# Attention scores in three float32r products: the lower parts of the keys on all 128 partitions, and one set of weights for both products of a score block

## The chip, the cores and the metric

The kernel runs on one core of a Trainium2 chip. The metric is the device time of one execution in microseconds (us). A profile is one execution taken by the hardware profiler; its times run from the first instruction of the program.

## What is computed

A backbone of two layers over 512 latent tokens and 256 context tokens of width 1024. Layer 0 mixes tokens by grouped-query attention (8 query heads, 2 key heads, 64 channels a head) beside a gated recurrence; layer 1 is an RWKV-7 mixer; each layer ends in a squared-ReLU MLP. The change lies in layer 0's attention alone:

```python
def attend(q, k, v):
    s = jnp.einsum('bqhgd,bkhd->bhgqk', q, k).astype(F32) * HEAD_DIM ** -0.5
    p = jax.nn.softmax(s, axis=-1).astype(v.dtype)
    return jnp.einsum('bhgqk,bkhd->bqhgd', p, v)

k_all = jnp.concatenate([kch, klh], axis=1)      # context keys, latent keys
att_l = blocked_attend(qlh, k_all, v_all)        # latents read all 768 keys
att_c = attend(qch, kch, vch)                    # context reads its 256 keys
```

## The kernel before

**Number format.** TensorE works here on float32r, whose products keep fewer bits than float32. So a float32 operand x is split into a high part hi (x as float32r) and a low part lo = x - hi, and a product of two such operands is made as a sum of products of parts. The dense products take three: hi hi, lo hi and hi lo (`mm3`, L270 to L276).

**Queries and keys.** `heads0` (L557) norms and rotates them, and its `stack` (L596 to L605) makes the parts. A tile of the stream holds two heads, one on partitions 0 to 63, the other on 64 to 127; `half(s)` is that half. For queries `stack` makes one tile a head, with hi on the head's own half of the partitions and lo, sent there by a DMA (L604), on the other half. For keys (`dup`) it makes one tile a head with hi on both halves, and one tile `kl` for both heads with each head's lo on its own half. ScalarE writes hi (L602), VectorE subtracts for lo (L603), SyncE's queue issues the DMAs (L604), and also those of the rotation (L591) that follow in the program.

**Scores.** `attention` (L625) goes through 12 units: four pairs of heads times three groups of query tiles (two groups of latents with 768 keys, one of context with 256 keys). Its generator `probs` (L632) makes four score tiles a unit (two heads, two query tiles of 128). A score tile is a PSUM tile `mm` with 768 or 256 columns, in segments of 512 and 256 columns, and a segment takes two products:

```python
self.mm(ps[:, c0:c1], q[j][s][:, qc], kd[s][:, c0:c1], True, False)   # L641
self.mm(ps[:, c0:c1], q[j][s][r, qc], kl[r, c0:c1], False, True)      # L642
```

The first contracts 128 rows (hi and lo of the queries with hi of the keys), the second the 64 rows of one half (hi with lo). In the trace both stand on L47, the helper `mm`: the first as `mm<-kq`, `128*128`, the second as `mm<-kl,kq`, `64*128` (rows times columns of the array). There are two `mm` tiles in PSUM (`mm2`, L71). A score tile is then read by VectorE for its row maximum (L645), by ScalarE for the exponential (L649), which is the last to read it, and the probabilities are scaled on GpSimd (L652).

**Values.** `values` (L656) transposes the probabilities (L663, `128*128`), copies them out (L666 on VectorE, L668 on ScalarE in turn) and multiplies them by the values (L671, in the trace on L47 as `aux<-pT,v`, `128*64`). The program interleaves the values of one unit with the scores of the next, and after each unit takes a step of other work (L688): a 1 MB block of modulation weights `ada_w` (L134, into one of two buffers `wst`), multiplied in small products (L136, `aux<-wst,cpad`, `128*32`). The compiler's scheduler orders each engine's instructions when the program is built; at run time each engine works its list in that order.

Before attention the last tiles of the input projection run on TensorE (`mm<-hhi,whi` and the like); after it the output projection (`mm<-mxh,whi`) starts.

Of the kernel before, what the change touches and what calls it, by code (L numbers as in the profile page):

```python
# [7 lines left out]
F32 = mybir.dt.float32  # L8
F32R = mybir.dt.float32r
# [6 lines left out]
P = 128  # L16
D = 1024
KT = 8
NL = 512
NC = 256  # L20
NT = NL + NC
# [13 lines left out]
class Net:  # L35
# [21 lines left out]
    @contextmanager  # L57
    def pool(self, name, side=None):
        """A pool for one part of the program; sb() allocates in the innermost."""
        old = self.sp  # L60
        with self.tc.tile_pool(name=name, bufs=1, side=side, reuse_waits="tile") as self.sp:
            yield self.sp
        self.sp = old
# [14 lines left out]
    def consts(self):  # L78
# [22 lines left out]
        # silu(c) = c/2 (1 + tanh(c/2)), the 2 rows padded with zeros to 32 columns  # L101
# [53 lines left out]
    def fill(self, n=1):  # L155
        """Emit n steps of the work that is waiting to be interleaved."""
        for _ in range(n):
            while self.todo:
                try:
                    next(self.todo[0])  # L160
                    break
                except StopIteration:
                    self.todo.pop(0)
# [5 lines left out]
    def ada_scale(self, l, j):  # L169
        """A = g (1 + scale) of norm j of layer l, for latents and context."""  # L170
        t = self.cp.tile([P, 2, KT], F32, name="A%d%d" % (l, j))
        for v in range(2):
            self.nc.vector.scalar_tensor_tensor(
                t[:, v, :], self.mod[l][:, v, (3 * j + 1) * KT:(3 * j + 2) * KT], 1.0,
                self.vec[:, VEC["g%d%d" % (l, j)], :], op0=OP.add, op1=OP.mult)
        self.A[l, j] = t
# [58 lines left out]
    def norm_split(self, l, j, ctx, parts, rb, tmp, ready=False):  # L235
        """In steps of a tile."""
# [33 lines left out]
    def mm3(self, ps, w, h, cols, first, last):  # L270
        """ps += w^T h by the three products of the parts."""
        (wh, wl), (hh, hl) = w, h
        c0, c1 = cols
        self.mm(ps, wh, hh[:, c0:c1], first, False)
        self.mm(ps, wh, hl[:, c0:c1], False, False)
        self.mm(ps, wl, hh[:, c0:c1], False, last)  # L276

    def gemm_tile(self, w, hi, lo, ctx, nk=KT):
        """One 128-row tile of (h W)^T for all tokens."""
# [7 lines left out]
    def gemm_pair(self, ws, hi, lo, ctx):  # L287
        """Two such tiles side by side, as h's tiles become ready."""
# [13 lines left out]
    def gemm_residual(self, l, chunk, blocks, hi, lo, pool, side, late, dest=None):  # L302
        """x += gate (h W), and the sums for the next norm. The context of the tiles from late on comes last, and between
        them what follows for the latents (side). These go to dest as well."""
# [22 lines left out]
    def mlp(self, l, ctx, parts, hpool):  # L327
        """parts: the normed stream, in a pool that is closed here. After layer 0's, the sums of squares of the
        stream are there."""
# [40 lines left out]
    def rg_consts(self):  # L370
# [5 lines left out]
        # softplus(-lam) = max(-lam, 0) + log1p(z), z = exp(-|lam|); log1p(z) = 2 atanh(z / (2 + z))  # L376
# [52 lines left out]
    def in_proj0(self, m, rb):  # L429
# [33 lines left out]
        # a tile of recurrent channels, then one of queries, four times  # L463
# [12 lines left out]
        with self.pool("m0pr"):  # L476
# [4 lines left out]
            # output gate of the recurrence  # L481
# [11 lines left out]
    def recurrence(self, i, ps, gw, m):  # L493
        """A tile of recurrent channels: centred convolution; gates, one scan per direction."""
# [62 lines left out]
    def heads0(self, qg, vT, pst):  # L557
        """Norm, rotation and float32r parts of queries, keys and values."""
# [6 lines left out]
        # 1 / rms of the heads, by token  # L565
# [30 lines left out]
        def stack(dup, x):  # L596
            """By head: parts of a half of the rows, with hi again (dup) or lo below; and lo where it was."""
            hs = [sb([P, NT], F32R, "kq", 10) for _ in range(2)]
            lo = sb([P, NT], F32R, "kl") if dup else self.sb([P, NT], F32, "tmp", 3, pool=self.mi).bitcast(F32R)
            for s, t in enumerate(hs):  # L600
                h, o = self.half(s), self.half(1 - s)
# [3 lines left out]
            return hs, lo  # L605
# [19 lines left out]
    def attention(self, rec, heads, mx):  # L625
        """By two tiles of queries of two heads; the heads' products side by side on the array."""
# [3 lines left out]
        groups = ((0, 0, NT), (2, 0, NT), (4, NL, NC))      # first query tile, first key, keys  # L630

        def probs(j, g, pr):  # L632
            qt0, kc0, nk = g
            for s in range(2):
                r, head = self.half(s), 2 * j + s
                for qt in range(qt0, qt0 + 2):
                    ps = self.mm2()
                    qc = slice(qt * P, qt * P + P)
                    for c0, c1, _ in self.segs(True):
                        if c0 >= kc0:  # L640
                            self.mm(ps[:, c0:c1], q[j][s][:, qc], kd[s][:, c0:c1], True, False)  # L641
                            self.mm(ps[:, c0:c1], q[j][s][r, qc], kl[r, c0:c1], False, True)  # L642
# [60 lines left out]
    def tm_norm_pool(self):  # L703
        self.rctx.append(self.wpool("l1n"))
        p = self.rctx[-1].__enter__()
        self.nb = self.sb([P, KT, NT], F32, "nb1", pool=p)       # sum of the neighbours
        self.rb = self.sb([P, NT], F32, "rb", pool=p)

    def tm_norm(self, seg, *tag):
        """The modulated norm, in place of the stream, and the sums of its tokens' neighbours."""  # L710
# [12 lines left out]
    def tm_project(self, keep):  # L723
        """The context's norm, token shift and the projections, and from them by pair of heads what the scan takes: to
        DRAM."""
# [23 lines left out]
        # two sets of parts; one is partly where the values' inputs will be  # L749
# [18 lines left out]
        # the low-rank sides of decay, in-context rate and gate, beside the keys  # L768
# [30 lines left out]
        # keys and their heads' norms  # L799
# [43 lines left out]
    def tm_pairs(self, vin, lw):  # L843
        """By pair of heads: loads (A), low rank products by direction (B0, B1), exponentials (C0, C1), products (D0, D1)
        and L (E0, E1). Then the values' projection, with the first inverses."""
        nc = self.nc
        with self.psum("l1e") as self.pq:
# [24 lines left out]
            # decays by step: the backward direction's a step ahead  # L872
# [24 lines left out]
    def tm_values(self, vin):  # L897
        """Values by token, to DRAM."""
        nc = self.nc
        xh, xl = [self.sb([P, NT], F32R, "vxh", KT, pool=self.vp) for _ in range(KT)], []  # L900
        for b in range(4):
# [4 lines left out]
            if b == 0:  # L906
                # an input's lower part in place of the input before
# [4 lines left out]
            for t0, tn in ((4, 2), (0, 4)) if b else ((0, 4), (4, 2)):  # L912
                ps = self.ps([P, 1024], "mmb", 2, pool=self.pq)
                for kt in range(KT):
                    for t in range(tn):
                        c = slice((t0 + t) * P, (t0 + t + 1) * P)
                        o = ps[:, 256 * t:256 * t + 256]
                        self.mm(o, xh[kt][:, c], wh[:, kt], kt == 0 and t % 2 == 0, False)    # two tiles share a bank
# [8 lines left out]
    def tm_prep_consts(self):  # L927
# [3 lines left out]
        # decayed keys come from k (s1 - s0 t), t = -tanh  # L931
# [5 lines left out]
    # A chunk has 64 tokens; 0-7 are latents, 8-11 context. In the scan, for direction d, the rows of a chunk's values  # L937
    # (by token) are on partitions 64 d on; those of its U, and its keys, queries and state by channel, on the other
    # half; the two heads of a pair lie side by side. The delta rule's queries are kk / sqrt 2, its keys -(tanh + 1)
    # times that; U is scaled to match.  # L940
    def tm_prep(self, kt, lw):
        """A pair of heads' decayed keys, queries and their products."""
# [13 lines left out]
        # normalised kk  # L956
# [8 lines left out]
        for d in range(2):  # L965
# [15 lines left out]
            # decay since the chunk's start and its inverse, for the sum before the token too  # L981
# [9 lines left out]
        for d in range(2):  # L991
# [20 lines left out]
            if d:  # L1012
                # the bonus' factor of v by token: r . (k both directions) r_k
# [35 lines left out]
    def tm_feed(self, i, KB=None, W=None):  # L1049
        """What step i needs besides the inverses, in pieces."""  # L1050
# [20 lines left out]
        for g in range(4):  # L1071
# [10 lines left out]
            if i:  # L1082
                # queries to go with the state
# [15 lines left out]
    def tm_invert(self, j):  # L1099
        """(I - L)^-1 of the chunks of steps 2 j and 2 j + 1: the diagonal 32 x 32 blocks by forward substitution,  # L1100
        chunks on partitions. The backward direction's L is upper triangular; its transpose goes the same way."""
        nc = self.nc
        XT = self.XT[j] = self.sb([P, 2, 2, KT, 64], F32, "XT", 3, pool=self.ip)      # step, head of a pair, pair, token
# [20 lines left out]
    def tm_below(self, j):  # L1124
        """The block below the diagonal: X22 L21 X11. In pieces, two for each of the two steps."""
# [30 lines left out]
    def tm_step(self, i, kt):  # L1156
        """Step i of the scan of a pair of heads."""
# [60 lines left out]
    def tm_post(self, l, parts=1):  # L1218
        """Group norm (but its shift), scale and bonus of chunks l and 7 - l, for all heads; from Y, by token, to Y, by channel."""
# [40 lines left out]
    def tm_masks(self):  # L1260
# [8 lines left out]
        self.GL = sb([P, 32, 32], F32, "GL")   # token, unit  # L1269
# [3 lines left out]
    def tm_scan(self):  # L1273
# [5 lines left out]
        # queries by channel, with zeros for the other direction's  # L1279
# [65 lines left out]
    def out1_ahead(self):  # L1345
        """Loads of the gate's and half of the output's weights, to where inverses were."""
# [22 lines left out]
    def out1(self, wo):  # L1369
        """Gate, output projection and residual: the inner 256 tokens, then the outer ones."""  # L1370
# [54 lines left out]
def layout(inp):  # L1425
    """The arrays of setup_inputs() as the program takes them: reordered, nothing computed."""
# [29 lines left out]
    # a head's channels: the first of every rotary pair, then the second  # L1456
# [20 lines left out]
    # layer 1  # L1477
# [3 lines left out]
    up = np.zeros((2, HD, 2, 2, D), np.float32)     # zeros in the rows of the other direction  # L1481
# [43 lines left out]
```

## Time and profile before

| | us |
|---|---|
| device time, three runs | 2335.08, 2324.70, 2331.64 |
| median | 2331.64 |
| span of the profiled execution | 2334.9 |
| TensorE busy in it | 2069.8 (89%) |
| VectorE, ScalarE, GpSimd busy | 1188.5, 870.0, 525.8 |
| attention, first to last score product | 239.70 to 391.8 |

The span of the profiled execution is 0.1% above the median of the runs. "PE" is TensorE, "PEld" its weight loads, "DVE" VectorE, "ACT" ScalarE, "POOL" GpSimd, "SPq" SyncE's queue. The duration that the trace gives for a matmul includes a modelled drain that lies under the next one; what a matmul takes of TensorE's time is the distance from its start to the start of the next. PEclk is the granted clock of TensorE as a share of 2.4 GHz, so that 0.50 is the lower level, 1.2 GHz.

### The profile page before, as it was taken

How to read it: one execution, taken by the hardware profiler on the slowest of the kernel's cores; microseconds unless marked ns; L12 is line 12 of the kernel's file. 1: busy time of each engine (PE TensorE's matmuls, PEld its weight loads, DVE VectorE, ACT ScalarE, POOL GpSimd, SP SyncE). 2: the span in 40 equal slices, each digit the busy share in tenths (PEclk: the TensorE clock that was granted, in tenths of full speed). 3: DMA queues.
4: the chain of work that ended last, by engine and by line, in shares of the span. 5: the costliest groups of instructions: out<-in, count | busy, mean ns of one | idle time of the engine just before them, and what ended most of it. 6: DMA issues, size and time to landing. Idle time of an engine off the chain costs nothing. (4 is left out here: it accounts for less than half of the span.)

```text
span 2334.9 us, 37318 instructions
## 1 busy us (share of the span) xinstructions
PE 2069.8 (89%) x15710; PEld 1639.0 (70%) x15710; DVE 1188.5 (51%) x1835; ACT 870.0 (37%) x1333; POOL 525.8 (23%) x530
## 2 busy tenths in 40 slices
PE   6888999999999999997987768578877878999999
PEld 3567445778888888875764558567756667788887
DVE  4557455262222222328648998638766584333333
ACT  3664344142121221317645542245534432332331
POOL 0123222011010110105005872660510130210210
PEclk8999789999999999998998778789888889999999
DMA  7324221123333212212224568286465330223222
GB/s 274 126 99 135 102 108 55 54 86 132 108 109 116 83 55 73 95 44 74 91 90 169 215 238 160 52 140 115 73 102 110 74 118 19 91 92 103 95 91 90
DMA packets 231784, 248.54 MB, mean 106 GB/s; under 512 B 52416, under 2 KB 209472, under 8 KB 225216
## 3 DMA queue, kind: packets, MB, share of 16 engines
q1 hardware_dynamic: 229568, 240.91, 35.5%
q0 software_dynamic: 896, 3.15, 0.4%
q8 instruction: 123, 2.02, 0.4%
q10 hardware_dynamic: 1152, 2.10, 0.2%
q14 instruction: 45, 0.37, 0.1%
HBM read 200.82 MB, written 41.94 MB: 104 GB/s over the span
## 5 line engine op out<-in xcount | busy, mean ns | idle before, releaser
L264 ACT ACTIVATE whi<-wst 128x1024 fp32r<-128x1024 f32 x160 | 169.2, 1059 | 583.6 <-PE mm L47 566.2
L47 PE MATMUL mm<-hhi,whi 128*128 128x512 f32 (+1 forms) x992 | 347.2, 357 | 14.5 <-ACT hhi L250 7.5
L47 PE MATMUL mm<-hlo,whi 128*128 128x512 f32 (+1 forms) x992 | 352.7, 356 | 2.2 <-DVE hlo L251 2.1
L47 PE MATMUL mm<-hhi,wlo 128*128 128x512 f32 (+1 forms) x992 | 350.3, 354 | 0.0
L265 DVE TENSOR_TENSOR wlo<-wst,whi 128x1024 fp32r<-128x1024 f32 x160 | 200.1, 1253 | 253.6 <-ACT whi L264 250.8
L345 POOL TENSOR_TENSOR mp<-mr 128x768 f32<-128x768 f32 (+1 forms) x64 | 109.9, 1718 | 841.5 <-ACT mr L344 841.5
L47 PE MATMUL mm<-ahi,wlo 128*128 128x512 f32 (+1 forms) x704 | 253.0, 359 | 0.0
L47 PE MATMUL mm<-ahi,whi 128*128 128x512 f32 (+1 forms) x704 | 252.9, 360 | 0.0
L47 PE MATMUL mm<-alo,whi 128*128 128x512 f32 (+1 forms) x704 | 252.6, 359 | 0.0
L300 DVE SCALAR_TENSOR_TENSOR Xt<-mm,mod,Xt 128x512 f32<-128x512 f32 (+1 forms) x112 | 70.6, 652 | 337.0 <-PE mm L47 337.0
L47 PEld LDWEIGHTS mm<-hhi,whi 128*128 128x128 f32 x992 | 188.2, 191 | 52.8 <-ACT hhi L250 9.5
L47 PEld LDWEIGHTS mm<-hlo,whi 128*128 128x128 f32 x992 | 189.1, 191 | 31.3 <-DVE hlo L251 5.7
L47 PEld LDWEIGHTS mm<-hhi,wlo 128*128 128x128 f32 x992 | 188.8, 190 | 29.1 <-issue 1.7
L47 PEld LDWEIGHTS mm<-ahi,whi 128*128 128x128 f32 x704 | 132.2, 188 | 28.1 <-issue 6.7
L47 PEld LDWEIGHTS mm<-ahi,wlo 128*128 128x128 f32 x704 | 132.5, 188 | 22.0 <-DVE wlo L265 1.1
L47 PEld LDWEIGHTS mm<-alo,whi 128*128 128x128 f32 x704 | 132.4, 188 | 21.9
L47 PE MATMUL mm<-QZ,KB 128*128 128x256 f32 (+1 forms) x384 | 97.7, 411 | 48.9 <-DMA KB<-kbr 22.7
L47 PEld LDWEIGHTS mm<-QZ,KB 128*128 128x128 f32 x384 | 74.6, 229 | 60.8 <-issue 37.5
L347 DVE TENSOR_TENSOR alo<-mp,ahi 128x768 fp32r<-128x768 f32 (+1 forms) x64 | 54.9, 857 | 113.0 <-ACT ahi L346 112.8
L1079 DVE TENSOR_TENSOR G<-mm,gmask 128x1024 f32<-128x1024 f32 (+1 forms) x48 | 51.0, 1062 | 94.7 <-PE mm L47 94.6
L346 ACT ACTIVATE ahi<-mp 128x768 fp32r<-128x768 f32 (+1 forms) x64 | 47.3, 739 | 110.3 <-POOL mp L345 110.2
L1086 ACT ACTIVATE G<-QZ 64x256 f32<-64x256 f32 x88 | 36.5, 415 | 114.6 <-DVE G L1079 113.5
(462 smaller groups left out, 4346.5 us busy)
## 6 DMA issues: line engine op xcount, KB each, us to landing
wst<-in_mlp_w_dram SPq DMA_DIRECT2D x64, 1024.0 KB, 5.3
wst<-in_ada_w_dram SPq DMA_DIRECT2D x48, 1024.0 KB, 5.8
kbr<-KB SPq DMA_DIRECT2D x16, 768.0 KB, 4.2
KB<-kbr SPq DMA_DIRECT2D x48, 256.0 KB, 5.8
wst<-in_rw_w_rkv_dram SPq DMA_DIRECT2D x8, 1024.0 KB, 5.4
qlr<-ql SPq DMA_DIRECT2D x16, 512.0 KB, 4.3
QZ<-qlr SPq DMA_DIRECT2D x16, 512.0 KB, 8.2
wst<-in_hy_w_in_dram SPq DMA_DIRECT2D x7, 1024.0 KB, 5.2
```

Of the source, the lines that this page charges most:

```text
L47: self.nc.tensor.matmul(out, lhsT, rhs, start=start, stop=stop)
L264: nc.scalar.activation(hi, w, AF.Copy)
L265: nc.vector.tensor_sub(lo, w, hi.bitcast(F32))
L300: self.nc.vector.scalar_tensor_tensor(x, ps[:, c0:c1], self.m(l, chunk, v, kt), x, op0=OP.mult, op1=OP.add)
L345: nc.gpsimd.tensor_mul(p[:, :n], r[:, :n], r[:, :n])
L346: nc.scalar.activation(h[:, :n], p[:, :n], AF.Copy)
L347: nc.vector.tensor_sub(o[:, :n], p[:, :n], h[:, :n].bitcast(F32))
L1079: nc.vector.tensor_mul(G.rearrange("p k n d t -> p (k n) d t"), ps[:, :8 * m].rearrange("p (k d t) -> p k d t", d=2, t=m), self.gmask[:, : ...
L1086: nc.scalar.activation(G[h, :, :, d, 0:64], QZ[h, 2 * g:2 * g + 2, :, d, 0:64], AF.Copy)
```

## The change

The low parts of the keys get one tile a head, with the same values on both halves of the partitions; a second DMA a head copies them to the other half. The second product of a segment then contracts 128 rows: hi and lo of the queries with lo of the keys, so the product lo lo, which was left out, is added. Its stationary operand (weights) is the one of the first product, `q[j][s][:, qc]`. The numbers of instructions on the compute engines stay; two DMAs of 192 KB are added. All other lines of the diff remove comments.

```diff
         def stack(dup, x):
             hs = [sb([P, NT], F32R, "kq", 10) for _ in range(2)]
-            lo = sb([P, NT], F32R, "kl") if dup else self.sb([P, NT], F32, "tmp", 3, pool=self.mi).bitcast(F32R)
+            lo = None if dup else self.sb([P, NT], F32, "tmp", 3, pool=self.mi).bitcast(F32R)
+            los = [sb([P, NT], F32R, "kl", 2) if dup else lo for _ in range(2)]
             for s, t in enumerate(hs):
-                h, o = self.half(s), self.half(1 - s)
+                h, o, lo = self.half(s), self.half(1 - s), los[s]
                 nc.scalar.activation(t[h], x[h], AF.Copy)
                 nc.vector.tensor_sub(lo[h], x[h], t[h].bitcast(F32))
                 nc.sync.dma_start(t[o].bitcast(F32), (t if dup else lo)[h].bitcast(F32))
-            return hs, lo
+                if dup:
+                    nc.sync.dma_start(lo[o].bitcast(F32), lo[h].bitcast(F32))
+            return hs, los
...
-                r, head = self.half(s), 2 * j + s
+                head = 2 * j + s
...
                             self.mm(ps[:, c0:c1], q[j][s][:, qc], kd[s][:, c0:c1], True, False)
-                            self.mm(ps[:, c0:c1], q[j][s][r, qc], kl[r, c0:c1], False, True)
+                            self.mm(ps[:, c0:c1], q[j][s][:, qc], kl[s][:, c0:c1], False, True)
```

## Rows read from the trace of the kernel before

**Rows 1.** The page, busy time by engine over the span.

```profile
PE 2069.8 (89%) x15710; PEld 1639.0 (70%) x15710; DVE 1188.5 (51%) x1835; ACT 870.0 (37%) x1333; POOL 525.8 (23%) x530
```

**Rows 2.** Table by stretch: start:end, length, busy (instructions) by engine, PEclk, DMA share, GB/s.

```profile
239.70:252.00 12.30, 8.63 (x43) 2.22 (x41) 4.57 (x8) 4.41 (x7) 2.72 (x2) 0.78 0.59 206
252.00:277.20 25.20, 25.20 (x71) 13.13 (x68) 10.59 (x26) 8.72 (x17) 5.65 (x7) 0.50 0.17 67
277.20:301.10 23.90, 22.17 (x108) 11.64 (x108) 14.51 (x33) 11.76 (x26) 8.40 (x11) 1.00 0.00 1
301.10:311.30 10.20, 10.20 (x35) 5.77 (x34) 3.63 (x8) 3.00 (x7) 2.31 (x3) 0.50 0.00 0
...
318.10:321.60 3.50, 3.50 (x15) 3.05 (x15) 2.23 (x5) 1.25 (x3) 1.65 (x3) 0.51 0.00 0
321.60:365.90 44.30, 42.38 (x234) 19.85 (x234) 24.77 (x57) 21.54 (x44) 12.00 (x15) 1.00 0.59 207
365.90:369.30 3.40, 3.40 (x17) 1.73 (x16) 1.55 (x4) 1.33 (x3) 1.33 (x2) 0.51 0.30 98
...
sum 152.10, PE 143.02 PEld 73.19 DVE 79.08 ACT 67.72 POOL 44.73; mean PE 15.89 PEld 8.13 DVE 8.79 ACT 7.52 POOL 4.97
```

**Rows 3.** TensorE's timeline at PEclk 1.00: start, duration, line, out<-in, rows*columns, count.

```profile
239.11 0.39 PE L47 MATMUL mm<-hhi,wlo 128*128 128x512 f32 x1
239.34 0.28 PE L47 MATMUL mm<-hhi,whi 128*128 128x256 f32 x1
239.46 0.28 PE L47 MATMUL mm<-hlo,whi 128*128 128x256 f32 x1
...
290.73 0.50 PE L47 MATMUL mm<-kq 128*128 128x512 f32 x1
291.16 0.50 PE L47 MATMUL mm<-kl,kq 64*128 64x512 f32 x1
291.59 0.39 PE L47 MATMUL mm<-kq 128*128 128x256 f32 x1
291.90 0.38 PE L47 MATMUL mm<-kl,kq 64*128 64x256 f32 x1
```

**Rows 4.** TensorE's timeline at PEclk 0.50, in attention and in a dense product.

```profile
254.43 0.79 PE L47 MATMUL mm<-kq 128*128 128x512 f32 x1
255.15 0.79 PE L47 MATMUL mm<-kl,kq 64*128 64x512 f32 x1
...
1067.95 0.63 PE L47 MATMUL mm<-vx,whi 128*128 128x512 f32 x1
1068.37 0.63 PE L47 MATMUL mm<-xhi,wlo 128*128 128x512 f32 x1
```

**Rows 5.** Groups by shape, 232 to 410 us: count | busy us, mean ns | idle before.

```profile
L47 PE MATMUL mm<-kl,kq 64*128 64x256 f32 x48 | 20.3, 422 | 0.0
L47 PE MATMUL mm<-kl,kq 64*128 64x512 f32 x32 | 18.0, 563 | 0.0
```

**Rows 6.** Timeline of VectorE and ScalarE: maximum and exponential of one score tile.

```profile
257.00 0.96 DVE L645 TENSOR_REDUCE sm<-mm 128x1 f32<-128x768 f32 x1 [1.32 <-PE mm L47]
258.25 0.99 ACT L649 ACTIVATE prob<-mm,sm,rq 128x768 f32<-128x768 f32 x1 [1.38 <-DVE sm L647]
```

**Rows 7.** Waits on TensorE's timeline in attention: [idle before <- what ended it].

```profile
247.40 1.94 PE L47 MATMUL aux<-wst,cpad 128*32 128x512 f32 x8 [2.91 <-DMA wst<-in_ada_w_dram]
...
300.38 0.49 PE L47 MATMUL mm<-kq 128*128 128x512 f32 x1 [0.85 <-ACT prob L649]
...
317.44 0.65 PE L47 MATMUL aux<-pT,v 128*64 128x256 f32 x4 [1.01 <-ACT pT L668]
...
363.95 0.51 PE L47 MATMUL mm<-kq 128*128 128x512 f32 x1 [1.18 <-ACT prob L649]
```

**Rows 8.** Ahead of attention: a key DMA on SyncE's queue, and TensorE's wait.

```profile
206.43 0.54 SPq L604 DMA_DIRECT2D kq<-kq  x1
...
218.79 0.50 PE L47 MATMUL mm<-hhi,whi 128*128 128x512 f32 x1 [3.08 <-ACT tmp L485]
```

## The prediction

> **What bounds the kernel now.** I read the page first, for the engine that sets the pace over the whole span: TensorE, busy 89%, with VectorE at 51% behind it [rows 1]. Then the table by stretch over attention, since the change lies there alone. From 239.7 to 391.8 us TensorE is busy 143.0 of 152.1 us, VectorE 79.1 and ScalarE 67.7 [rows 2]: TensorE's list is the bound, nearly without a hole. But that busy share hides two losses. The first is the clock: it is at 0.50 from 252 to 277.2, 301.1 to 311.3, 318.1 to 321.6 and 365.9 to 369.3, in all 42 us [rows 2]. The second is seen only in TensorE's own timeline, by distances from start to start. At the full clock a dense product of 512 columns takes 0.23 us (239.11 to 239.34) and one of 256 columns 0.12 (239.34 to 239.46). A score product of the same columns takes 0.43 (290.73 to 291.16, 291.16 to 291.59) and 0.31 (291.59 to 291.90) [rows 3]. Each is some 0.193 us longer, whatever its length. What differs is that the score products alternate between 128 and 64 rows, and the dense ones stay at 128*128. At the half clock it is 0.72 (254.43 to 255.15) against 0.42 (1067.95 to 1068.37), so 0.295 us more [rows 4]. I read this as the price of a change of shape: the next product does not start into the array while the last one is in it. Last I looked at the chain that hands a score tile back (maximum, exponential) and at the waits, for what is late next.
>
> **Changes of shape removed.** There are 80 pairs of score products, 32 with 512 columns and 48 with 256 [rows 5]. Each pair has one change inside it: 80. After the second product comes another one of 128*128 (the first of the next segment, or a transposition) in 32 pairs of 512 columns and 17 of 256; behind the other 31 come values (128*64) or modulation (128*32), where the change stays. So 129 go. Counted along TensorE's timeline, from the first score product at 239.70 to the last at 391.50, they fall into four parts:
>
> - Before 251.96: 6, at the full clock. Modulation waits there for its weights (2.91 us at 247.40) [rows 7], so most is hidden. Only what the first tile saves (3 x 0.193) passes on, since the freed buffer's load is issued that much earlier: 0.6 us.
> - 251.96 to 264.83: 19 at the half clock, worth 19 x 0.295 = 5.6 us of TensorE. Here five score tiles follow each other almost without other work, 2.57 us apart. There are two `mm` tiles, so a tile can't start before the exponential of the one before the last has read its own. The last product of a tile, started at 256.38, ends about 256.89; its maximum runs from 257.00, its exponential from 258.25 to 259.24 [rows 6]: 2.35 us. With the products at 2 x 0.43 + 2 x 0.21 = 1.3 us (0.21 is an estimate, half of the 512 columns' 0.43) and a change or a transposition at 0.2, the period is (2.35 + 1.5) / 2, about 1.95 us. So VectorE and ScalarE become the bound, and the five tiles give 5 x 0.62 = 3.1 us, not 5.6.
> - Behind it 12 at the half clock: 3.5 us.
> - Behind it 92 at the full clock: 17.8 us.
>
> In these last two parts transpositions and values lie between the score tiles, and TensorE's list stays the longest: 126 us of it less 21.3, against some 75 us of VectorE [rows 2]. But each engine works its list in order, and TensorE already waits six times there for an exponential or a copy (0.85, 1.01 and 1.18 us are three of them) [rows 7]; of the 9.1 us in which it idles in attention [rows 2] these are 5.4, the rest are waits for modulation weights. A faster TensorE meets the same chains earlier. From below the extra waiting is nothing (both come earlier by the same amount), from above 16 us (0.4 us at each of some 40 tiles). I take a doubling of the present waits, 5.4 us, because they are the nearest rows. These parts then give 15.9 us.
>
> **The weights.** Loads of weights are no term. In the dense product each product has its own load and still takes 0.12 us [rows 3], so the same weights for both products bring nothing beyond the shape that they share, and the same shape is enough. The Trainium skill speaks against this: "TensorE: Matmul & The Clock Gate", Part 3 (packing small matmuls), has a weight load overlap a running matmul only when the two use different row groups. By it full-row products could not follow each other as closely as I count; that is the second rival below. The dense rows speak against it, at 0.12 us apart with all rows in use.
>
> **The clock.** The long half-clock stretch that ends at 277.2 begins when TensorE has waited for modulation weights, which the change does not touch, and ends only after values and transpositions alone have run for some microseconds. With the score products closer together I expect it to end earlier, by 0 to 20 us; I take 8. At the half clock the same work takes nearly twice as long (0.42 against 0.23 for 512 columns), in attention's mixture some 1.8 times, so 8 us give 3.6.
>
> **The lo lo part** costs nothing of its own: 64 and 128 rows take the same time from start to start (0.43 and 0.43) [rows 3].
>
> **The two DMAs.** Each costs 0.54 us of SyncE's queue [rows 8], and waits there for VectorE's subtraction. Behind it stand the rotation's DMAs of the queries (L591), 1.1 to 2.1 us later then. GpSimd and VectorE wait for these, then ScalarE, and behind that in ScalarE's list stands the copy for which TensorE waits 3.08 us at 218.79 [rows 8]. VectorE's own work covers most of it; without that cover it is 2 us. Bounds 0 and 2; I take 0.5. The copied halves themselves land some 27 us before the first score product needs them, so their landing is hidden.
>
> **Sum.** 0.6 + 3.1 + 15.9 + 3.6 - 0.5 = 22.7 us. The profiled span of 2334.9 becomes 2312.2; the median of the runs, 3.3 lower, becomes 2309. What follows attention is paced by its own work and only shifts.
>
> **Rivals.**
>
> 1. The chains take it. If each of some 40 tiles behind 265 us waits 0.4 us longer for VectorE and ScalarE, 16 us of the 21.3 go instead of 5.4, and the kernel takes about 2320. For it: VectorE rises to 75% of attention, with copies and reductions in one list. Against it: transpositions and values lie ready to fill. Chance 0.13.
> 2. Full-row products don't follow closely. If the 0.193 us stays because the two products still exclude each other, nothing is gained and the DMAs cost 0.5: 2332. This is where the skill's rule on row groups leads. Against it: the dense products [rows 3]. Chance 0.05.
> 3. The clock takes it and more: slower. In the rows a wait for the `mm` tiles or a copy is followed by the half clock: the wait before 300.38 by the stretch from 301.1, that before 317.44 by 318.1, that before 363.95 by 365.9 [rows 2, 7]. If a faster TensorE waits at most tiles, the clock may stay low. The full-clock stretches come to 97.5 us, 79.7 after the change; each of these that falls to the half clock costs some 0.75 us. From 30 us on the gain is gone, at 46 the kernel is 11.8 us slower; I price it at 50: 2346. The same page's part on depth-cycling of the PSUM queue describes this, a clock that swings when TensorE idles briefly between groups. Against it: the same columns in less time, and holes only where they already are. Chance 0.08.
> 4. The clock gives much more. If all but the first 10 us behind 252 run at the full clock, the 36 us of half-clock work that are left become 20, and 15 us come instead of 3.6: 2298. Chance 0.12.
>
> **How the numbers follow.** The forecast has a chance of 0.62. A measurement of this kernel can tell 0.5%, 11.7 us, from no change. Faster by more holds the forecast, the fourth rival and 0.05 of the first: 0.79. Within it lie 0.08 of the first and the second: 0.13. Slower is the third: 0.08. The range reaches from near the fourth's time, 2296, to 2326, where the chains take nearly all; outside stay the slower case, the second rival and the tails.
>
> **What would show it.** After the change a 256-column score product should start 0.12 us before the next at the full clock, and a 512-column one 0.23, with about 0.31 only ahead of values or modulation. A distance of 0.31 throughout makes the second rival right. Attention's first to last score product should shrink from 152 us to 129, with TensorE's waits for L649 and L668 grown from 5.4 to some 11. Waits of 20 us or more mean the first rival; a granted clock of 0.50 over more than 70 us of attention the third, under 25 us the fourth. TensorE's wait near 218.79 should stay between 3 and 5 us.

## The result and the profile after

| | before | after |
|---|---|---|
| device time, median (us) | 2331.05 (2324.70 to 2335.08, 4 runs) | 2292.73 (2291.28 to 2294.50, 4 runs) |
| ratio, 95% interval | | 0.9838 (0.9820 to 0.9857) |
| span of the profiled execution | 2334.9 | 2289.5 |
| up to the first score product | 239.7 | 243.0 |
| attention, first to last score product | 151.8 | 121.1 |
| from there to layer 1's first projection | 671.2 | 670.2 |
| layer 1, first projection to last product of the scan | 821.3 | 804.6 |
| behind it | 450.9 | 450.5 |

The kernel became 38.3 us faster, where 22.7 were forecast, and the time lies 3 us below the range. The two spans differ by 45.4 us: 30.7 in attention and 16.7 in layer 1, a stage 670 us behind attention that shares no line with the diff; ahead of attention 3.3 went the other way. Attention's part is read first.

The page of after, busy time by engine: TensorE has the same 15710 instructions as in [rows 1] and 39.7 us less to do.

```profile
PE 2030.1 (89%) x15710; PEld 1627.8 (71%) x15710; DVE 1179.8 (52%) x1835; ACT 869.2 (38%) x1333; POOL 524.1 (23%) x530
```

The table by stretch of after, with the columns of [rows 2]: the whole of attention, and the one stretch in it that is at the lower clock.

```profile
242.90:364.40 121.50, 105.67 (x667) 62.30 (x665) 78.61 (x185) 66.60 (x139) 44.59 (x51) 0.94 0.32 113
249.00:262.70 13.70, 10.39 (x36) 5.53 (x36) 8.00 (x18) 5.14 (x10) 3.62 (x4) 0.50 0.63 233
```

In [rows 2] TensorE was busy for 143.0 of 152.1 us; now for 105.7 of 121.5. It lost 37.3 us of work time and idles 6.7 us longer (15.8 against 9.1). The three later stretches at 0.50 in [rows 2] are gone.

TensorE's timeline of after, first at the full clock (the place of [rows 3], then a tile that follows transpositions), then at the lower one ([rows 4]).

```profile
280.56 0.50 PE L47 MATMUL mm<-kq 128*128 128x512 f32 x1
280.90 0.40 PE L47 MATMUL mm<-kl,kq 128*128 128x512 f32 x1
281.13 0.28 PE L47 MATMUL mm<-kq 128*128 128x256 f32 x1
281.25 0.28 PE L47 MATMUL mm<-kl,kq 128*128 128x256 f32 x1
281.46 0.65 PE L47 MATMUL aux<-pT,v 128*64 128x256 f32 x4
...
284.45 0.77 PE L666 MATMUL aux<-ident,prob 128*128 128x128 f32 x5
284.97 0.48 PE L47 MATMUL mm<-kq 128*128 128x512 f32 x1
285.28 0.39 PE L47 MATMUL mm<-kl,kq 128*128 128x512 f32 x1
...
256.22 0.63 PE L47 MATMUL mm<-kq 128*128 128x512 f32 x1
256.64 0.63 PE L47 MATMUL mm<-kl,kq 128*128 128x512 f32 x1
257.07 0.41 PE L47 MATMUL mm<-kq 128*128 128x256 f32 x1
257.29 0.41 PE L47 MATMUL mm<-kl,kq 128*128 128x256 f32 x1
```

From start to start, inside a tile: 0.23 (280.90 to 281.13) for 512 columns and 0.12 (281.13 to 281.25) for 256, the distances of the dense products in [rows 3]; at the lower clock 0.43 and 0.22. Where the shape still changes, to values of 64 columns, 0.21 is left for 256 columns (281.25 to 281.46); coming back from them the first product takes 0.34 for 512 (280.56 to 280.90). So a change from 128*128 to 128*64 costs the product ahead of it about 0.1. The 0.1 on the way back can't be put down to the shape alone: behind transpositions, which have its own shape, the first product takes 0.31 too (284.97 to 285.28).

What TensorE waits for in attention of after, grouped: who waits <- who ended it: us in all, count, longest. The rows answer to [rows 7].

```profile
PE aux L47 <- ACT pT L671: 5.2, 7, 1.2
PE aux L47 <- DMA wst<-in_ada_w_dram: 5.1, 4, 3.2
PE mm L47 <- ACT prob L652: 3.8, 4, 1.4
PE aux L666 <- ACT pT L671: 0.7, 1, 0.7
PE aux L666 <- POOL prob L655: 0.6, 1, 0.6
```

Without the DMAs these are 10.3 us (5.2 + 3.8 + 0.7 + 0.6).

### The profile page after: what moved, and what is told of

The parts are those of the page before. It is cut to its first block, busy times and chain, and to the rows that moved or that the text cites. A ratio compares the mean times of both kernels' runs of the same rounds, so it can differ in the third digit from the quotient of the medians.

```text
span 2289.5 us, 37320 instructions
## 1 busy us (share of the span) xinstructions
PE 2030.1 (89%) x15710; PEld 1627.8 (71%) x15710; DVE 1179.8 (52%) x1835; ACT 869.2 (38%) x1333; POOL 524.1 (23%) x530
## 5 line engine op out<-in xcount | busy, mean ns | idle before, releaser
L47 PE MATMUL sc<-W,G 128*64 128x64 f32 (+1 forms) x1280 | 67.9, 233 | 17.6 <-DVE S L1194 15.1
```

Of the source, the lines that this page charges most:

```text
L47: self.nc.tensor.matmul(out, lhsT, rhs, start=start, stop=stop)
```

## The experiments

The theory, A in the texts, has three parts: the changes of row count and the clock that comes with their going give attention's 25 to 30 us; layer 1 is faster because its instructions stand in another order, which the compiler's scheduler chose anew; and the two added DMAs take 3 us back in the wait ahead of attention. Its rival, B: the whole gain is attention's, and the difference in layer 1 has nothing to do with the order; it comes from an earlier start, or is only how one execution differs from another. Each kernel was timed against before on its chip; before's medians there were 2331.7 (the first four), 2330.3 (the next three) and 2333.7 us (the last two).

**Rows alone, without the DMAs and the second tile.** On before:

```diff
-                            self.mm(ps[:, c0:c1], q[j][s][r, qc], kl[r, c0:c1], False, True)
+                            self.mm(ps[:, c0:c1], q[j][s][:, qc], kl[:, c0:c1], False, True)
```

> The kernel before with one edit: the second score product takes all 128 rows of the old single tile kl, in which the other half of the partitions holds the other head's lower part (a spurious term of the size lo times lo). No DMA is added. Theory A (three parts: a fixed price of 0.19 us for each change between 64 and 128 rows; a wait ahead of attention that the two added DMAs make 3 us longer; and a layer 1 whose instructions the scheduler puts into another order): attention from first to last score product takes 121 us as in the changed kernel (152 before), it starts at 239.7 us as before and not at 243.0, and layer 1, in a third order, takes 800 to 825 us from its first projection product to its last scan product; the total is 2290 to 2310. Theory B (the whole gain is attention's, and layer 1 is faster because the rest comes earlier): layer 1 takes 800 us as in the changed kernel, 2288 to 2291 in all.

**The same rows, other weights.** On after:

```diff
-                            self.mm(ps[:, c0:c1], q[j][s][:, qc], kl[s][:, c0:c1], False, True)
+                            self.mm(ps[:, c0:c1], q[j][1 - s][:, qc], kl[s][:, c0:c1], False, True)
```

> The changed kernel with one edit: the second score product takes the other head's query tile as weights, so the two products of a segment have the same shape but different weights (the scores' small term is then of the wrong head). All instructions stand in the order of the changed kernel. If only the shape matters: score products 0.23 and 0.12 us apart at the full clock, attention 121 us, 2293 +- 3 in all, and layer 1 again 800 +- 3 us, since its order is the same. If the shared weights save a load: each second product 0.05 to 0.19 us longer, attention 4 to 15 us longer, 2297 to 2308. If layer 1's 17 us were chance from one execution to the next, its time here lies anywhere between 800 and 817.

**The DMAs alone, with 64 rows in the second product.** On after:

```diff
-                            self.mm(ps[:, c0:c1], q[j][s][:, qc], kl[s][:, c0:c1], False, True)
+                            self.mm(ps[:, c0:c1], q[j][s][r, qc], kl[s][r, c0:c1], False, True)
```

> The changed kernel with its added tile and DMAs, but the second score product takes 64 rows as before. Theory A: score products 0.43 and 0.31 us apart at the full clock and attention 152 us as before; TensorE's wait near 220 us grows from 3.1 to 6.1 us, attention starts at 243.0; layer 1 has an order of its own, 800 to 825 us; 2318 to 2340 in all. Theory B: layer 1 takes 817 us as before, 2334 to 2336 in all. If the added DMAs were harmless, attention starts at 239.7.

**64 rows in both products.** On before:

```diff
-                            self.mm(ps[:, c0:c1], q[j][s][:, qc], kd[s][:, c0:c1], True, False)
+                            self.mm(ps[:, c0:c1], q[j][s][r, qc], kd[s][r, c0:c1], True, False)
```

> The kernel before with the first score product, too, on the 64 rows of a head's own half (the term of the queries' lower part is left out of the scores). If it is the change between 64 and 128 rows that costs: score products 0.23 and 0.12 us apart inside a tile, with 0.31 to 0.43 only where a transposition or values stand next; attention 125 to 135 us. If full rows are what makes the products fast (or what keeps the clock up): the distances stay at 0.31 and 0.43, or the clock stays at 0.50 for more than 40 us of attention, and attention takes 145 us or more.

| | median (us) | ratio, 95% interval | attention | of it at 0.50 | layer 1 |
|---|---|---|---|---|---|
| rows alone | 2290.11 | 0.9839 (0.9810 to 0.9868) | 122.2 | 10.2 | 800.9 |
| other weights | 2289.27 | 0.9835 (0.9807 to 0.9862) | 120.4 | 6.8 | 802.0 |
| DMAs alone | 2322.84 | 0.9960 (0.9937 to 0.9983) | 147.2 | 37.5 | 812.2 |
| 64 rows in both | 2298.24 | 0.9868 (0.9839 to 0.9897) | 126.0 | 20.5 | 806.1 |

TensorE's timeline, first with other weights (with the weight load of the second product of 256 columns), then with 64 rows in both, then with the DMAs alone (all at the full clock):

```profile
278.85 0.50 PE L47 MATMUL mm<-kq 128*128 128x512 f32 x1
279.19 0.40 PE L47 MATMUL mm<-kl,kq 128*128 128x512 f32 x1
279.43 0.28 PE L47 MATMUL mm<-kq 128*128 128x256 f32 x1
279.54 0.28 PE L47 MATMUL mm<-kl,kq 128*128 128x256 f32 x1
279.66 0.27 PE L666 MATMUL aux<-ident,prob 128*128 128x128 f32 x1
...
279.43 0.19 PEld L47 LDWEIGHTS mm<-kl,kq 128*128 128x128 f32 x1
```

```profile
282.33 0.39 PE L47 MATMUL mm<-kl,kq 64*128 64x512 f32 x1
282.57 0.28 PE L47 MATMUL mm<-kq 64*128 64x256 f32 x1
282.68 0.27 PE L47 MATMUL mm<-kl,kq 64*128 64x256 f32 x1
282.89 0.65 PE L47 MATMUL aux<-pT,v 128*64 128x256 f32 x4
```

```profile
288.29 0.50 PE L47 MATMUL mm<-kq 128*128 128x512 f32 x1
288.73 0.50 PE L47 MATMUL mm<-kl,kq 64*128 64x512 f32 x1
289.15 0.39 PE L47 MATMUL mm<-kq 128*128 128x256 f32 x1
289.47 0.38 PE L47 MATMUL mm<-kl,kq 64*128 64x256 f32 x1
```

Three things follow. With other weights a product of 256 columns still starts 0.11 to 0.12 us before the next (279.43, 279.54, 279.66), and the time is that of after: the shared weights bring nothing. With 64 rows in both the distance is 0.11 too: full rows bring nothing either, it is the change of row count that costs. That kernel still changes the row count where transpositions stand next to score products: between the first and the last score product TensorE changes its shape 142 times there, 231 times in before and 101 times with full rows. Its attention is 3.8 us longer than that of the rows alone. And the DMAs alone leave the old distances (0.44, 0.42, 0.32) and the old attention. On layer 1 the rows alone don't decide: their 2290.1 us and 800.9 in layer 1 lie within what both theories expected. The DMAs alone speak against B, which wanted 817 us there and 2334 to 2336 in all.

The third part of theory A fell. TensorE's wait ahead of attention, near the 218.79 of [rows 8], in after, then with the rows alone, then with the DMAs alone:

```profile
221.34 0.79 PE L47 MATMUL mm<-hhi,whi 128*128 128x512 f32 x1 [6.11 <-ACT tmp L485]
```

```profile
221.97 0.79 PE L47 MATMUL mm<-hhi,whi 128*128 128x512 f32 x1 [6.13 <-ACT tmp L485]
```

```profile
218.54 0.50 PE L47 MATMUL mm<-hhi,whi 128*128 128x512 f32 x1 [2.64 <-ACT tmp L485]
```

It is 6.1 us in the kernel without the added DMAs and 2.6 in one with them, so the DMAs don't make it. With other weights, where the program is that of after up to attention, it is 4.0 us and attention starts at 240.5, not 243.0, so it differs from execution to execution:

```profile
218.81 0.80 PE L47 MATMUL mm<-hhi,whi 128*128 128x512 f32 x1 [4.00 <-ACT tmp L485]
```

Ahead of it stands VectorE's wait for the rotation's DMA, in after and with the rows alone:

```profile
204.80 0.69 DVE L593 TENSOR_TENSOR qg<-qg,rope 128x512 f32<-128x512 f32 x1 [6.72 <-DMA tmp<-qg]
```

```profile
205.26 0.69 DVE L593 TENSOR_TENSOR qg<-qg,rope 128x512 f32<-128x512 f32 x1 [6.58 <-DMA tmp<-qg]
```

These waits move with the landing of the 1 MB load of `hy_w_in` ahead of them: it landed at 203.9 in after and 204.4 with the rows alone, at 202.1 with other weights, at 200.9 in before and 201.2 with the DMAs alone. What delays that load was not tried.

**Layer 1.** Between the kernels the compiled program differs in layer 1 too, without an edit there: the same instructions, in another order. Of the kernels so far before has one order, after and other weights a second, the rows alone a third, and the other two have orders of their own. To change the order and leave the scores as they are, transpositions that nobody reads were added between attention and the MLP of layer 0. Of 56 and 68 on before, the first leaves layer 1 in before's order, and the second gives it the order of the rows alone. Of 76 and 12 on the rows alone, the first gives before's order and the second keeps its own. A further kernel is before with one comment reworded, for the spread between profiles.

```diff
+        pad = self.aux()
+        for _ in range(56):
+            self.nc.tensor.transpose(pad[:, :P], self.ident, self.ident)
         self.mlp(0, True, *mid)
```

> The kernel before once more, with a comment changed, for a second trace of it. If layer 1's 821 us (first projection product to last scan product; 801 to 812 in the five other kernels) belong to the order of its instructions, it takes 816 to 826 again. If they were chance of one execution, it takes 800 to 812. Attention takes 148 to 153 us, by how long the clock stays at 0.50.

> The kernel before with 56 transpositions of 128 by 128 put behind attention, ahead of the MLP (0.109 us each at the full clock, 6.1 us). The scheduler leaves layer 1 in the order of the kernel before. A control for the next one: before plus 6 us, 2334 to 2341, and layer 1 as in the kernel before (816 to 826 if the order sets it).

> The same with 68 transpositions (7.4 us). Scores are as before, with 64 rows in the second product, but at this length the scheduler puts layer 1 into the order that it has in the kernel with one kl tile. If that order is what makes layer 1 faster: layer 1 801 us +- 4 and 8 to 18 us less than the run with 56, 2318 to 2330. If layer 1's gain comes from the scores or from the clock after them: 1.3 us more than the run with 56, and layer 1 as there.

> The kernel with one kl tile (128 rows in both score products, no added DMA) with 76 transpositions behind attention (8.3 us). At this length the scheduler puts layer 1 of it into the order of the kernel before, on every engine. If that order costs the 12 to 17 us by itself: layer 1 takes 814 to 822 us, 2308 to 2316 in all, some 21 us more than the run with 12 transpositions. If the new scores make layer 1 faster in whatever order: 799 to 806 us and some 7 us more than the run with 12.

> The same with 12 transpositions (1.3 us), at which layer 1 keeps the order that it has with one kl tile and no padding: layer 1 799 to 806 us, attention 120 to 123 us, 2289 to 2293 in all.

| | median (us) | ratio, 95% interval | attention | of it at 0.50 | layer 1 | its order |
|---|---|---|---|---|---|---|
| before, comment reworded | 2327.84 (one run) | | 146.4 | 34.1 | 818.7 | before's |
| before + 56 | 2339.09 | 1.0034 (1.0017 to 1.0051) | 147.0 | 37.5 | 821.8 | before's |
| before + 68 | 2325.86 | 0.9979 (0.9962 to 0.9996) | 147.6 | 37.5 | 809.2 | of the rows alone |
| rows alone + 76 | 2311.64 | 0.9907 (0.9885 to 0.9930) | 122.5 | 10.2 | 817.5 | before's |
| rows alone + 12 | 2289.61 | 0.9820 (0.9796 to 0.9845) | 122.1 | 10.2 | 803.5 | of the rows alone |

Layer 1 in the table by stretch, of before + 56, before + 68, rows alone + 76, rows alone + 12:

```profile
1063.20:1885.00 821.80, 654.04 (x8160) 533.85 (x8160) 579.22 (x880) 386.68 (x663) 305.84 (x365) 0.86 0.49 118
```

```profile
1065.50:1874.60 809.10, 647.86 (x8158) 532.61 (x8160) 567.51 (x880) 386.73 (x663) 301.37 (x365) 0.86 0.50 120
```

```profile
1041.40:1858.90 817.50, 648.42 (x8158) 529.23 (x8160) 578.84 (x880) 386.91 (x663) 306.61 (x365) 0.87 0.49 119
```

```profile
1033.50:1836.90 803.40, 640.71 (x8158) 525.84 (x8160) 567.79 (x880) 386.37 (x663) 301.35 (x365) 0.86 0.51 121
```

By order these are 817.5 and 821.8 against 803.4 and 809.1; by scores 809.1 and 821.8 against 803.4 and 817.5. The order is worth 12.7 us with the old scores and 14.1 with the new ones, at the same instruction counts and mean granted clocks of 0.86 and 0.87. The medians say the same. 64 transpositions are worth 6.4 us (the stage from attention to layer 1 has 677.6 us with 76 and 671.2 with 12), 0.1 each. From 56 to 68 the time falls by 13.2 us although 1.2 are added: 14.4. From 76 to 12 it falls by 22.0, of which 6.4 are transpositions: 15.6. So theory B is refuted: the order alone is worth 13 to 16 us. An earlier start is not it: with 76 transpositions layer 1 begins 22 us before that of before + 56 and takes 817.5 us all the same. Nor is it the clock: layer 1 is at 0.50 for 217.3 us with 76 and for 217.0 with 12. Two numbers were missed: layer 1 of before + 68 was expected at 801 us and took 809.1, and attention of the second profile of before at 148 to 153 and took 146.4.

One place where the orders part is seen in the low-rank products of layer 1 (group, count: starts of the first instructions and the last; the last two times are the first and the last start), in before + 56 and before + 68:

```profile
L47 PE MATMUL mmb<-lw,ust x128: 379/592/1222, 1236.7 to 1378.7; 128*128 128x512 f32 x64, 128*128 128x256 f32 x64
```

```profile
L47 PE MATMUL mmb<-lw,ust x128: 379/592/1220, 1239.0 to 1361.1; 128*128 128x512 f32 x64, 128*128 128x256 f32 x64
```

The last starts 315.5 us behind layer 1's start in the one (1378.7 - 1063.2) and 295.6 in the other. From 470 to 620 us behind that start, in the same two kernels:

```profile
1533.20:1683.20 150.00, 123.07 (x1984) 103.72 (x1984) 99.69 (x215) 75.30 (x161) 53.64 (x87) 0.84 0.59 99
```

```profile
1535.50:1685.50 150.00, 128.22 (x2180) 107.52 (x2178) 102.69 (x223) 81.56 (x175) 57.32 (x97) 0.86 0.60 98
```

TensorE gets through 196 products more there in before + 68, where the scan has begun. Which of the exchanged instructions is the cause stays open.

## Why the prediction came out as it did

**The price of a change of shape** was right, and so was the count: 129 changes were to go, and 130 went (231 to 101). Inside a tile the products came to 0.23 and 0.12 us as forecast, and no weight load held them up. Ahead of values 0.31 was forecast and 0.21 came, in the kernel with 64 rows in both as well (282.68 to 282.89): that product now has a change on one side only. The first product of 512 columns behind values or transpositions takes 0.31 to 0.34, where 0.23 was forecast. The sentence of the Trainium skill ("TensorE: Matmul & The Clock Gate", Part 3) that a load overlaps a running product only in another row group is contradicted here: with other weights and all rows in use, 256 columns follow each other 0.12 us apart, although each load takes 0.19 us. The same Part also lets a load into a background buffer go ahead, and that would agree. The Trainium skill's "TensorEngine Tiling (Array Packing)", Key Properties, says that a change of the tiling mode drains TensorE; that agrees with 0.31 against 0.12 us for 256 columns between 64 and 128 rows.

**Attention as a whole** was forecast to give 23.2 us, from 152 to 129. In the two profiles it gave 30.7. But before's profile is the longest of the five with the old scores: the others have 146.4 to 147.6, and the five kernels with full rows 120.4 to 122.5. From the middle of those four (147.0) to that of these five (121.5) it is 25.5 us, 2 us more than forecast. In the kernels with full rows the scheduler ordered attention's own instructions anew too (values stand right behind a score product 22 times there, 26 times in before). The kernel with 64 rows in both has before's order in attention but for a few instructions, and its 126.0 us are 21 less; how much of the last 4.5 the new order gives was not separated.

**The extra waits** were right: 10.3 us where a doubling to 10.8 was forecast. The waits for modulation weights, taken as unchanged, grew by 1.4 us (3.7 to 5.1). The first rival, the chains, wanted 16 us more and didn't come.

**The clock** was mis-sized. I took 8 us less at 0.50, so that some 34 of the 42 us in [rows 2] would stay; 13.7 stayed. The fourth rival's mark (under 25 us) was the one that was met. All kernels with alternating row counts have 34 to 48 us of attention at 0.50 (before itself 47.8, with the part of its first stretch in [rows 2] that the mean of 0.78 hides), those with full rows 7 to 14, and the one with 64 rows in both 20.5. In the profiled pair, attention's 30.7 us lie near the 34.1 of that rival (22.7 - 3.6 + 15). The third rival, a clock that stays low, was wrong in its sign.

That attention as a whole came so near its forecast is in part luck. Take the DMAs alone and after, whose programs differ in the rows of the second product; the row is that of the DMAs alone, with the columns of [rows 2]:

```profile
240.20:387.40 147.20, 138.22 (x665) 70.42 (x663) 78.76 (x185) 67.36 (x139) 44.44 (x51) 0.87 0.27 94
```

Attention falls by 26.1 us (147.2 to 121.1), the time at 0.50 by 23.8 (37.5 to 13.7), and TensorE idles 6.8 us longer (9.0 to 15.8). At the prediction's own rate, 3.6 us for 8, the clock gave 10.7, an estimate. The changes of shape are left with some 22.2 (26.1 + 6.8 - 10.7), where 25.0 were forecast (0.6 + 3.1 + 3.5 + 17.8). So a clock term 7 us too small stood against changes taken 3 us too high and waits taken 1 us too low.

**The DMAs**, forecast at 0.5 us, can't be seen: rows alone, without them, takes 2290.1 us, after 2292.7 and other weights, with them, 2289.3, and the intervals of their ratios overlap. My expectation that the wait near 218.79 would stay between 3 and 5 us failed (6.1), but not through the DMAs: with other weights, which has them, it is 4.0.

**The step that failed** is "What follows attention is paced by its own work and only shifts." Layer 1 became 16.7 us shorter in the profiles. With before's order in layer 1 the new scores (rows alone + 76) take 2311.6 us less 7.6 for the transpositions, about 2304, inside the range and 5 below the forecast. The rest of the way to 2292.7, some 11 us, is of the size that the order of layer 1's instructions is worth in the pairs above (12.7 to 15.6). For after's own order there is no kernel that has it with the old scores, so its share is inferred from those pairs, not measured.

What stays open: at one order the new scores are still faster in layer 1, by 4.3 us (821.8 to 817.5) in before's order and by 5.7 or 8.2 us (809.1 to 803.4 or 800.9) in that of the rows alone. The three profiles with before's order and scores spread over 3.1 us (818.7 to 821.8), so part of this may be spread.

## What to carry to other kernels

Look in TensorE's timeline at distances from start to start, not at busy time: products that alternate between row counts each lose some 0.2 us at the full clock, and giving them one row count, even with rows that hold almost nothing, wins that back, with either count tried (64 and 128) and whether or not they share weights. Where a scheduler orders the whole program, a local edit can reorder stages far away, so compare the time by stage and the instruction order before a gain is put down to the edit; padding that restores the old order separates the two.

## What was not expected of the hardware

The granted clock followed the alternation of row counts: 34 to 48 us of attention at 0.50 with it, 20.5 where it stayed only beside transpositions, 7 to 14 without it, with the same columns of work. What makes the clock follow was not tried. TensorE was busier with it (143.0 of 152.1 us in [rows 2] against 105.7 of 121.5) and yet at the lower clock for longer. In layer 1 VectorE's 880 instructions took 579 us in before's order and 568 in that of the rows alone, with the same work. Why a VectorE instruction takes longer in one order is open; the order as a whole is worth over half a per cent of the kernel's time (13 to 16 us).
